# Runs of four matmuls in one chunk, and the sums of two norms one chunk later and one chunk earlier

## The chip, the cores and the metric

One Trainium2 chip, of which the program uses one core. The time is device microseconds for one execution, from start to end, on that core. Shown is the median of three runs; one further execution was profiled.

## The reference

Two transformer blocks after one another, on 256 positions of width 2048, all in float32. Block 1 has a banded attention and a gated linear attention side by side, then a feed-forward of width 5632 with a causal convolution and gelu, then a gate with a side input (`ple`). Block 2 has a sliding-window attention and a stick-breaking attention, two gated branches, and a feed-forward of width 5632 without convolution. Cut to what the change touches:

```python
# block 1
x = x + (gelu(u_gate) * u_val) @ w_ffn_down            # u = conv(rms_norm(x) @ w_ffn_up)
h = rms_norm(x, norm_ple_w)
x = x + sigmoid(h @ w_ple_gate) * (p @ w_ple_proj)
x = rms_norm(x, final_norm_w)
# block 2
h = rmsnorm(x, norm_mix_g);  proj = h @ w_in           # attentions, branches, w_out
x = x + merged @ w_out
x = x + (silu(gate) * up) @ w_ffn_down                 # gate, up = split(rmsnorm(x, norm_ffn_g) @ w_ffn_in)
```

## The kernel before

**Chunks.** Every weight matrix is streamed through as chunks of 128 x 1024 numbers (512 KB), in one list `self.chunks`. A chunk is loaded (`load_ahead`, on SP's queue, up to five ahead) and split in two parts, `hi` (ACT rounds it to float32r, L195) and `lo` (DVE subtracts, L115), up to two chunks ahead of TensorE (three in `ple`), each in one of four buffers (`split`). The activations are split in the same way and stand side by side as 256 columns of hi and 256 of lo.

**Matmuls of a chunk.** A chunk of `job_t` has eight 128 x 128 tiles of weights (two output tiles `m` by four `kk`). Each tile makes two matmuls on L269: its `hi` part against all 512 columns and its `lo` part against the first 256. A hi and a lo result are added when they are evacuated from PSUM (`joined`, L330 on ACT and L115 on DVE). `multiply` sets their order: `runs = (2, 2, 2, 2)` means two tiles with hi, the same two with lo, and so on four times; a run is here one such group, hi and then lo.

**Pairs.** `pair_up(at, alone, odd)` takes a stretch of the list. Its first `alone` chunks stay single, with runs of two tiles. All others are taken two at a time in one run of sixteen tiles: sixteen hi, then sixteen lo; their hi part starts 15 numbers further into its buffer. `odd=True` gives the last single chunk `runs = (4, 2, 2)`, three runs for four. `w_out` of block 1 has two single chunks and `odd=True`. Each feed-forward has 264 chunks (176 of the first matrix and 88 of the second): ten single ones and 127 pairs, both with `odd=False`. The gates and branches of block 2 from the third on (36 pairs) and `w_out_2` (16 pairs) have no single chunk.

**Work between chunks.** After the matmuls of each chunk `step()` goes once through a list of generators (`hot`, the attention chains and others): each issues its instructions up to its next `yield`. `yield AGAIN` means a second go in the same step. What a chunk's `after` appends is first run in the step after the next chunk. Evacuations that need the factor of the norm wait until `self.inv` is set, and two are issued per step (`may_evac`). A chunk that opens a new output tile needs a free PSUM bank out of four; if there is none, `lin_tile` calls `step()` until one is free, with no matmul in between.

**The norms.** The sum over features of a norm is a matmul with ones (`norm_sums`, L394 and L397) of the sums of squares that POOL adds up in `acc` (L359, L361). `norm` yields `wait` times, issues the sum, then in the next step the first half of `rstd` (DVE, ACT with Ln and Exp) and in the step after it the second half (three DVE instructions), with which `inv` is set. `ev_res` starts it for the norm before the feed-forward of either block and for the one before `ple` (`norm_ple_w`). In the first chunks of `ple` the order is: three chunks of the gate's job 0, three of job 1, the fourth of job 0, the projection chunk of job 0, the fourth of job 1.

`norm_between` computes the two norms between the blocks at once: two sums, of `accs[0]` (squares of x before the gain) and `accs[1]` (after it). The first chunks of block 2 are, by `overlap`, `ak` 0 to 2, `av` 0 to 2, `ak` 3, `av` 3, then `aq` 0 and on. `ak` and `av` fill all four PSUM banks.

Of the kernel before, what the change touches and what calls it, by code (L numbers as in the profile page):

```python
# [91 lines left out]
class Builder:  # L92
# [602 lines left out]
    def ev_res(self, k0, src, wname, pool, tag, acc):  # L695

        def ev(m, ps):
            k = k0 + m
            self.add_res(k, ps)
            yield AGAIN  # L700
            x = self.xr[k]
            self.scaled_in(src, k, pool, tag, x, self.vec(wname, k))
            self.sum_squares(acc(), x, k == 0)
            if k == KD - 1:
                self.inv = None
                self.hot.append(self.norm(acc(), wait=2))
            yield
        return ev

# [204 lines left out]
    def ffn(self, wu, wd, conv):  # L914
        nc, a = self.nc, self.a
        h = self.h_ffn
        segs = ((0, 16), (16, 16), (32, 12))
        top = len(self.chunks)
        acc = []
        out = Src(KD)  # L920
        self.h_next = out
        st = {}

        def conv_of(ps, j):
            while not self.may_evac():
                yield
            t = self.joined(ps)
            u = self.ft.tile([P, T], F32, tag="cu", name="cu")
            nc.gpsimd.tensor_tensor(u, t, self.inv[:, :T], ALU.mult)  # L929
            yield  # L930
            if not conv:
                return u
            o = self.ft.tile([P, T], F32, tag="co", name="co", bufs=4)
            self.act(o, u, AF.Identity, scale=self.vec("conv2", j), bias=self.vec("b_ffn_conv", j))
            self.stt(o[:, 1:], u[:, :T - 1], self.vec("conv1", j), o[:, 1:], ALU.mult, ALU.add)
            self.stt(o[:, 2:], u[:, :T - 2], self.vec("conv0", j), o[:, 2:], ALU.mult, ALU.add)
            yield
            return o

        for si, (f0, fn) in enumerate(segs):  # L940
            g = Src(fn)

            def ev_gate(j0):
                def ev(m, ps):
                    o = yield from conv_of(ps, j0 + m)
                    gt = self.ft.tile([P, T], F32, tag="gt", name="gt", bufs=4)
                    self.act(gt, o, AF.Gelu_apprx_tanh if conv else AF.Silu)
                    st[j0 + m] = gt
                return ev

            def ev_val(j0, g=g, f0=f0):
                def ev(m, ps):
                    o = yield from conv_of(ps, KF + j0 + m)
                    j = j0 + m
                    gt = st.pop(j)
                    self.tt(gt, gt, o, ALU.mult, nc.gpsimd if conv else None)
                    self.put_y(g, j - f0, gt)
                return ev

            at = len(self.chunks)  # L960
            for j in range(f0, f0 + fn, 2):
                self.job_t(wu, 0, KD, j // 2, h, ev_gate(j))
                self.job_t(wu, 0, KD, (KF + j) // 2, h, ev_val(j))
            if si == 0:
                self.overlap(at, 4)
            final = si == len(segs) - 1

            def ev_down(k0, final=final):
                def ev(m, ps):
                    self.add_res(k0 + m, ps)  # L970
                    yield
                return ev
            at = len(self.chunks)
            for j in range(KD // 2):
                if not final:
                    ev = ev_down(2 * j)
                elif conv:
                    ev = self.ev_res(2 * j, out, "norm_ple_w", self.xa, "xa", lambda: acc[0])
                else:
                    ev = self.ev_final(2 * j)  # L980
                before = None
                if final and j == 0:
                    def before():
                        acc.append(self.new_acc())
                        self.acc_f = acc[0]
                        if conv:
                            self.open_ple()
                self.job_t(wd, f0, fn, j, g, ev, before=before)
            self.overlap(at, fn // 4)
        self.pair_up(top, 10, odd=False)  # L990


    def open_ple(self):
# [73 lines left out]
    def norm_between(self, accs):  # L1067

        nc = self.nc
        inv = self.const.tile([P, 258], F32, tag="inv", name="inv", bufs=2)
        i1 = self.ft.tile([P, T], F32, tag="inv1", name="inv1", bufs=1)
        m1 = self.ft.tile([P, 258], F32, tag="m1", name="m1", bufs=1)
        yield
        yield
        pb = self.bank2(1)
        p1 = self.norm_sums(accs[0], pb[:, 0], True)  # L1080
        p2 = self.norm_sums(accs[1], pb[:, 1], True)
        yield

        def both(m):
            self.mean_eps(p1, D)(m1)
            nc.vector.tensor_scalar(m, m1, scalar1=EPS, scalar2=None, op0=ALU.mult)
            self.stt(m, p2, 1.0 / D, m, ALU.mult, ALU.add)
        yield from self.rstd(inv, both, 258)
        self.inv = inv
        for _ in range(4):  # L1090
            yield
        yield from self.rstd(i1, lambda m: nc.vector.tensor_copy(m, m1[:, :T]), T)
        for k in range(KD):
            nc.gpsimd.tensor_tensor(self.xr[k], self.xr[k], i1, ALU.mult)
            if k % 2:
                yield
# [368 lines left out]
```

## Time and profile before

| what | value |
|---|---|
| median of 3 runs | 2601.51 us (2599.85 to 2602.99) |
| profiled execution, time | 2602.29 us |
| its span, first to last instruction | 2600.6 us |
| TensorE's matmuls (PE) busy | 2578.5 us, 99% of the span |
| weight loads (PEld) busy | 2239.1 us, 86% |
| DVE, ACT, POOL busy | 65%, 52%, 21% |
| mean granted TensorE clock | 0.998 |

A busy PE is not PE at its peak: matmuls overlap, and the profile models their ends. The pace is read from the distance between the starts of rows. The profiled execution is 0.8 us above the median, and 1.7 us of its time lie outside the span.

### The profile page before, as it was taken

To read this page: it belongs to the slowest core of one execution; us is meant where nothing else is said; L and a number is where in the kernel's file an instruction comes from. 1 tells how busy PE (TensorE), PEld (TensorE's weight loads), DVE (VectorE), ACT (ScalarE), POOL (GpSimd) and SP (SyncE) were. 2 spreads that over 40 slices of the span, in tenths; PEclk is the share of its full clock that TensorE was granted. 3 is DMA by queue.
4 is the path that set the end of the run, shared out by engine and by line. 5 is a ranking of instruction groups with operands and counts; after the bars stand their busy time and mean duration, and the time that the engine had idled before them with its cause. 6 is when DMAs were issued, how large, how long until landed. Compare 5 with 4: busy or idle time off the path is not lost.

```text
span 2600.6 us, 39330 instructions
## 1 busy us (share of the span) xinstructions
PE 2578.5 (99%) x14864; PEld 2239.1 (86%) x14864; DVE 1692.3 (65%) x2241; ACT 1346.4 (52%) x2018; POOL 553.0 (21%) x638
## 2 busy tenths in 40 slices
PE   9999999999999999999999999999999999999997
PEld 7888888888888888888878888888888888888886
DVE  7457677776677667779676665556655555555555
ACT  5545545664466446557555655554554444444443
POOL 4121232220122012346520121112211001100114
PEclk9999999999999999999999999999999999999999
DMA  7556565666566656655545555656555555555553
GB/s 247 155 163 190 168 232 189 194 194 195 190 194 193 195 190 193 224 165 166 167 144 156 154 178 188 194 193 190 185 192 186 188 182 191 192 182 192 185 188 122
DMA packets 133753, 480.38 MB, mean 185 GB/s; under 512 B 15067, under 2 KB 17371, under 8 KB 133436
## 3 DMA queue, kind: packets, MB, share of 16 engines
q1 hardware_dynamic: 132108, 474.45, 57.3%
q8 instruction: 117, 1.92, 0.3%
q0 software_dynamic: 736, 2.36, 0.3%
q10 hardware_dynamic: 720, 1.06, 0.1%
q14 instruction: 72, 0.59, 0.1%
HBM read 475.71 MB, written 2.10 MB: 184 GB/s over the span
## 4 chain that ended last, share of the span: by engine, by line
PE 96%; DVE 1%; POOL 1%; DMA 1%; issue 0%; ACT 0%; DVEq 0%; SPq 0%; ACTq 0%
PE lin L269 87%; PE lin L311 4%; PE lin L309 2%; PE c L269 1%; PE c L792 1%; PE c L742 1%; PE c L779 0%; DMA raw<-in_w_out 0%; DVE lo L115 0%; PE c L1282 0%; DMA raw<-in_w_gk 0%; DVE x L115 0%; POOL x_in L525 0%; PE c L891 0%; PE c L872 0%
## 5 line engine op out<-in xcount | busy, mean ns | idle before, releaser
L115 DVE TENSOR_TENSOR lo<-raw,hi 128x1024 fp32r<-128x1024 f32 (+1 forms) x889 | 1104.0, 1275 | 658.8 <-issue 330.5
L195 ACT CAST hi<-raw 128x1024 fp32r<-128x1024 f32 (+1 forms) x890 | 912.7, 1046 | 480.0 <-PE lin L269 424.7
L269 PE MATMUL lin<-xa,hi 128*128 128x512 f32 x3808 | 985.1, 393 | 0.8 <-DVE xa L118 0.4
L269 PEld LDWEIGHTS lin<-xa,hi 128*128 128x128 f32 x3808 | 668.2, 188 | 107.9 <-issue 2.3
L269 PE MATMUL lin<-g,hi 128*128 128x512 f32 x2592 | 665.0, 394 | 3.4 <-DVE jo L115 3.1
L269 PEld LDWEIGHTS lin<-xa,lo 128*128 128x128 f32 x3808 | 534.5, 188 | 59.9 <-DVE lo L115 5.2
L269 PE MATMUL lin<-xa,lo 128*128 128x256 f32 x3808 | 549.4, 279 | 1.1 <-DVE lo L115 1.1
L269 PEld LDWEIGHTS lin<-g,hi 128*128 128x128 f32 x2592 | 458.3, 188 | 80.8 <-issue 6.1
L269 PEld LDWEIGHTS lin<-g,lo 128*128 128x128 f32 x2592 | 358.8, 188 | 35.0 <-DVE lo L115 0.4
L269 PE MATMUL lin<-g,lo 128*128 128x256 f32 x2592 | 366.8, 279 | 0.0
L929 POOL TENSOR_TENSOR cu<-jo,inv 128x256 f32<-128x256 f32 x176 | 128.2, 749 | 1113.0 <-DVE jo L115 1113.0
L330 ACT COPY jb<-lin 128x256 f32<-128x256 f32 x313 | 113.2, 371 | 70.7 <-PE lin L269 58.4
L118 DVE SCALAR_TENSOR_TENSOR co<-cu,vecs,co 128x255 f32<-128x255 f32 (+1 forms) x176 | 89.7, 531 | 53.1 <-ACT co L112 50.0
L115 DVE TENSOR_TENSOR jo<-lin,jb 128x256 f32<-128x256 f32 x297 | 113.6, 417 | 11.7 <-ACT jb L330 8.9
L112 ACT ACTIVATE co<-cu,vecs 128x256 f32<-128x256 f32 x88 | 52.9, 602 | 103.9 <-POOL cu L929 99.9
L348 ACT CAST g<-gt 128x256 fp32r<-128x256 f32 x88 | 35.6, 404 | 115.1 <-DVE gt L115 89.2
L359 POOL TENSOR_TENSOR sq<-x 128x256 f32<-128x256 f32 x73 | 58.4, 800 | 150.5 <-DVE x L115 150.3
L361 POOL TENSOR_TENSOR acc<-acc,sq 128x256 f32<-128x256 f32 x73 | 89.0, 1219 | 5.7
L115 DVE TENSOR_TENSOR jo<-lin,x 128x256 f32<-128x256 f32 x128 | 53.3, 416 | 29.0 <-PE lin L269 28.8
L112 ACT ACTIVATE xa<-x,vecs 128x256 fp32r<-128x256 f32 x48 | 24.5, 510 | 86.9 <-DVE x L115 86.9
L269 PE MATMUL lin<-m,hi 128*128 128x512 f32 x256 | 62.3, 395 | 0.0
L1180 POOL TENSOR_TENSOR u<-jo,inv 128x256 f32<-128x256 f32 x32 | 24.1, 770 | 175.4 <-DVE jo L115 175.4
(217 smaller groups left out, 1622.9 us busy)
## 6 DMA issues: line engine op xcount, KB each, us to landing
raw<-in_w_ffn_up SPq DMA_DIRECT2D x176, 512.0 KB, 4.3
raw<-in_w_ffn_down SPq DMA_DIRECT2D x176, 512.0 KB, 4.3
raw<-in_w_ffn_in SPq DMA_DIRECT2D x176, 512.0 KB, 4.3
raw<-in_w_out SPq DMA_DIRECT2D x64, 512.0 KB, 4.4
raw<-in_w_aq SPq DMA_DIRECT2D x32, 512.0 KB, 3.7
raw<-in_w_ple_gate SPq DMA_DIRECT2D x32, 512.0 KB, 4.3
raw<-in_w_ga SPq DMA_DIRECT2D x32, 512.0 KB, 3.7
raw<-in_w_gb SPq DMA_DIRECT2D x32, 512.0 KB, 4.1
```

What stands on the lines that cost most here:

```text
L112: self.nc.scalar.activation(out, in_, func, **kw)
L115: (eng or self.nc.vector).tensor_tensor(out, a, b, op)
L118: self.nc.vector.scalar_tensor_tensor(out, in0=in0, scalar=scalar, in1=in1, op0=op0, op1=op1)
L195: self.nc.scalar.copy(hi, r)
L269: self.nc.tensor.matmul(ps[m][:, T:] if lo else ps[m], lhsT=(ch.lo if lo else ch.hi)[:, at:at + P], rhs=src.tile[k][:, :T] if lo else src. ...
L309: self.nc.tensor.matmul(ps[t][:, :wd], lhsT=xl, rhs=wt, start=k == 0, stop=False)
L311: self.nc.tensor.matmul(ps[t][:, :wd], lhsT=xh, rhs=wt, start=False, stop=bool(lo) and k == KD - 1)
L330: self.nc.scalar.copy(b[:n], ps[:n, T:])
L348: self.nc.scalar.copy(t[:, :T], x)
L359: g.tensor_tensor(sq, x, x, ALU.mult)
L361: g.tensor_tensor(acc, acc, sq, ALU.add)
L929: nc.gpsimd.tensor_tensor(u, t, self.inv[:, :T], ALU.mult)
```

## The change

The last of the ten single chunks of block 2's feed-forward gets runs of four, two and two tiles. The sum of the norm before `ple` is issued one step later, and the sums between the blocks one step earlier.

```diff
@@ ev_res
-                self.hot.append(self.norm(acc(), wait=2))
+                self.hot.append(self.norm(acc(), wait=3 if wname == "norm_ple_w" else 2))
@@ ffn
             self.overlap(at, fn // 4)
-        self.pair_up(top, 10, odd=False)
+        self.pair_up(top, 10, odd=not conv)
@@ norm_between
         m1 = self.ft.tile([P, 258], F32, tag="m1", name="m1", bufs=1)
-        yield
         yield
         pb = self.bank2(1)
```

`conv` is true for block 1's feed-forward and false for block 2's.

## Rows read from the trace of the kernel before

**Rows 1.** The page: the chain that ended last by engine; a group of matmuls.

```profile
PE 96%; DVE 1%; POOL 1%; DMA 1%; issue 0%; ACT 0%; DVEq 0%; SPq 0%; ACTq 0%
...
L269 PE MATMUL lin<-xa,lo 128*128 128x256 f32 x3808 | 549.4, 279 | 1.1 <-DVE lo L115 1.1
```

**Rows 2.** Windows of PE: the pairs of either feed-forward; length, busy (matmuls), clock, DMA.

```profile
437.60:1129.40 691.80, 691.80 (x4067) 1.00 0.61 196
...
1871.60:2585.30 713.70, 713.70 (x4066) 1.00 0.56 183
```

**Rows 3.** Timeline of PE, first pair of block 1's feed-forward: start, us.

```profile
437.44 0.39 PE L269 MATMUL lin<-xa,lo 128*128 128x256 f32 x2
437.66 3.80 PE L269 MATMUL lin<-xa,hi 128*128 128x512 f32 x16
...
443.11 3.79 PE L269 MATMUL lin<-xa,hi 128*128 128x512 f32 x16
```

**Rows 4.** The same, last single chunk and first pair of block 2's feed-forward.

```profile
1868.57 0.40 PE L269 MATMUL lin<-xa,lo 128*128 128x256 f32 x2
1868.81 0.62 PE L269 MATMUL lin<-xa,hi 128*128 128x512 f32 x2
...
1871.33 0.40 PE L269 MATMUL lin<-xa,lo 128*128 128x256 f32 x2
1871.57 3.90 PE L269 MATMUL lin<-xa,hi 128*128 128x512 f32 x16
...
1877.19 3.89 PE L269 MATMUL lin<-xa,hi 128*128 128x512 f32 x16
```

**Rows 5.** The same, the chunk with three runs in w_out of block 1.

```profile
322.45 0.40 PE L269 MATMUL lin<-g,lo 128*128 128x256 f32 x2
322.68 1.08 PE L269 MATMUL lin<-g,hi 128*128 128x512 f32 x4
...
325.24 0.39 PE L269 MATMUL lin<-g,lo 128*128 128x256 f32 x2
325.46 3.80 PE L269 MATMUL lin<-g,hi 128*128 128x512 f32 x16
```

**Rows 6.** The same, last attention matmuls of block 2 to its first pair.

```profile
1523.43 0.87 PE L792 MATMUL c<-l,vb 128*64 128x256 f32 x8
...
1525.50 0.39 PE L269 MATMUL lin<-g,lo 128*128 128x256 f32 x2
...
1557.46 3.80 PE L269 MATMUL lin<-g,hi 128*128 128x512 f32 x16
```

**Rows 7.** The same, a wait within the pairs of w_out of block 1.

```profile
342.20 3.87 PE L269 MATMUL lin<-g,hi 128*128 128x512 f32 x16 [0.23 <-DVE x L115]
345.90 2.05 PE L269 MATMUL lin<-g,lo 128*128 128x256 f32 x16
```

**Rows 8.** Timelines of POOL and PE at the norm before ple.

```profile
1140.65 1.59 POOL L361 TENSOR_TENSOR acc<-acc,sq 128x256 f32<-128x256 f32 x1
...
1141.13 0.39 PE L269 MATMUL lin<-xa,lo 128*128 128x256 f32 x2
1142.30 0.70 PE L394 MATMUL c<-acc,ones 128*128 128x256 f32 x2 [0.78 <-POOL acc L361]
```

**Rows 9.** Timelines of POOL, PE and DVE at the norms between the blocks; a window.

```profile
1246.85 1.81 POOL L361 TENSOR_TENSOR accb<-accb,sq 128x256 f32<-128x256 f32 x2
...
1252.57 0.59 PE L394 MATMUL c<-acc,ones 128*128 128x256 f32 x2
...
1254.41 0.43 DVE L404 TENSOR_SCALAR m<-c 128x258 f32<-128x258 f32 x1 [1.26 <-PE c L397]
...
1256.23 1.12 PE L311 MATMUL lin<-lo,g 128*128 128x256 f32 x8
1260.48 0.85 PE L269 MATMUL lin<-g,hi 128*128 128x512 f32 x2 [3.13 <-DVE jo L115]
...
1260.50:1264.10 3.60, 3.60 (x12) 3.07 (x13) 1.39 (x2) 1.36 (x3) 1.35 (x2) 0.55 0.27 108
```

## The prediction

> **What bounds the kernel.** I read the page first. The chain that ended last is 96% PE [rows 1], so time is won only where PE waits or where its matmuls come faster. Waits of PE are few, so the second view is the windows of its busy time, one for the 127 pairs of each feed-forward. Both windows hold the same work (4067 and 4066 matmuls recorded), both at full granted clock, and PE is never idle in them; yet block 1's takes 691.8 us and block 2's 713.7 [rows 2]. Fewer bytes per us move in the slower one, and no engine is waited for. The pairs themselves are slower: by the timeline, from one pair's first row to the next, 443.11 - 437.66 = 5.45 us in block 1 and 1877.19 - 1871.57 = 5.62 us in block 2 [rows 3, 4]. Sixteen hi matmuls last 3.80 us at the first pace and 3.90 at the second.
>
> So TensorE has two paces for the same matmuls. Read along the timeline they are a state that is handed on. A pair passes on the pace it was given. A single chunk alternates: its rows of two lo matmuls last 0.39 us at the fast pace and 0.40 at the slow, in turn, one run fast and one slow, so four runs leave the pace as they found it. What the pairs inherit is the last lo row before them: 0.39 in block 1 and the pairs are fast [rows 3]; 0.40 in block 2 and they are slow [rows 4]. What it is in the hardware the profile doesn't tell; I use it as a state that the rows show.
>
> **The change part by part.** *Three runs in the last single chunk.* No matmul, load or wait is added or removed; 16 matmuls change places. An odd number of runs should hand on the other pace. The trace has one such chunk, in w_out of block 1, and it stands where the new one will: the lo row before it is slow, 0.40 (322.45), as is the one before block 2's last single chunk (1868.57) [rows 4, 5]. It ends with a fast row, 0.39 (325.24), and the pair behind it is fast, 3.80 [rows 5]. The chunk itself takes 325.46 - 322.68 = 2.78 us, against 1871.57 - 1868.81 = 2.76 with four runs [rows 4, 5]: a loss of 0.02. The gain is 127 x (5.62 - 5.45) = 21.6 us by single pairs, 713.7 - 691.8 = 21.9 by windows. I take 21.9. The bounds are 0 (the pace isn't turned) and 21.9. That the faster pace can be fed follows from block 1's feed-forward, which holds it for all 127 pairs with the same loads (DMA share 0.61) and more work on DVE, ACT and POOL [rows 2].
>
> Here a rule speaks against the change. The Trainium skill ("TensorE: Matmul & The Clock Gate", section "Back-to-back issue gap") gives the distance of back-to-back matmuls at the full clock from their columns alone, N/2.4 ns plus about 2.5: 215.8 and 109.2 ns here, 5.20 us for a pair in any order. By it the edit is worth 0 and the sum is 5.0 us. This trace disagrees: the same 32 matmuls take 5.45 and 5.62 us.
>
> Would the norms' edits disturb the entry? They lie before block 2's attention. After its last attention matmuls the second lo row is already fast (0.39), only whole chunks of four runs follow, and the first pair is fast [rows 6]. The edits move whole steps between chunks, so I expect that stretch, and the singles of the feed-forward, to begin as now.
>
> *The norm before ple, one chunk later.* PE comes to the sum behind the chunk whose last lo row starts at 1141.13 and takes 0.22 [rows 3, 8], but POOL ends the last addition at 1140.65 + 1.59 = 1142.24, and the sum starts at 1142.30 [rows 8]. PE loses 1142.30 - 1141.13 - 0.22 = 0.95 us. One chunk later, some 2.76 us, POOL has long ended: 0.9 us won, between 0 (the next lo part is late instead) and 0.95. What is late next is `inv`, by one step: its second half is then issued in the step after the fourth chunk of the gate's job 0. That chunk's evacuations are first tried in the step behind it, when `inv` is set in both versions; so no evacuation is put off and the two jobs' four banks come free as before. Queued behind the delayed DVE and ACT work are the splits of chunks three ahead, which have two chunks of 2.76 us to spare. If that cover were gone, PE would wait for a bank here as it does at the next norm, up to 4.8 us.
>
> *The sums between the blocks, one chunk earlier.* Now PE issues them behind `ak` 3 (1252.57). DVE's first instruction on them starts 1254.41 - 1252.57 = 1.84 us later, and from there to the next matmul it is 1260.48 - 1254.41 = 6.07 us [rows 9]: Ln and Exp, a split, the second half of `rstd`, and the first joined tile, because all four banks are full until `inv` lets `ak` be evacuated. PE's last matmul before it is over at 1256.23 plus 8 x 0.12 (eight in 1.12 us, one lasting 0.28: 0.84/7) = 1257.19 [rows 1, 9]. It waits 3.29 us. Afterwards it has half the clock for a while: the window behind holds 12 matmuls in 3.60 us at 0.55, where six hi and lo at 2.76/8 would take 2.07 [rows 4, 9]: another 1.5 us.
>
> In the new place the sums start behind `av` 2, one chunk earlier, at 1252.57 - 2.76 = 1249.81. POOL's last addition to `accs[1]` ends at 1246.85 + 1.81 = 1248.66 [rows 9], 1.15 us before: a cover that holds if PE comes 0.9 earlier, and more since the second sum comes behind the first. The same chain then ends at 1249.81 + 1.84 + 6.07 = 1257.72; DVE may still be at three splits before it, which I allow 0.4 for. PE, whose work up to there is the same, still needs until 1257.19. A wait of 0.5 to 0.9 is left, I take 0.7: 2.6 us won, and 1.5 for the clock, which I expect not to fall after so short a wait. That is 4.1; bounds 0 (the attention chains give it back) and 4.8. `inv` is set before `aq` 0 in both versions (now by a forced step, then by an ordinary one), so everything behind it keeps its place by chunks, and moves up with PE, whose freed buffers pace the splits.
>
> **Sum.** 21.9 - 0.02 + 0.9 + 4.1 = 26.9 us, so 2602.3 - 26.9 = 2575.4 for the profiled execution. That one was 0.8 above the median, so I forecast 2574.6. Its own range takes the norms at 0 to 5.7, and 1.6 us of spread between runs: 2572 to 2581.
>
> **The rivals.** *The pace isn't turned.* Then only the norms count: 2601.5 - 5.0 = 2596.5. For it: the one chunk that shows the turn is in another stage, with other operands (`g`, not `xa`). The rule of the Trainium skill weighed above would be it, too. Against it: same shapes, same buffers and offsets, the same pace before it, and block 1's feed-forward, whose `xa` pairs are fast behind a fast row [rows 3].
>
> *The pace is turned and lost on the way.* In w_out of block 1 the fast pairs end at a wait of PE: the row at 342.20 has 0.23 us idle, the lo row behind it takes 2.05, and it stays at that [rows 7]. A single wait in the feed-forward, for a late lo part or bank, could do the same. Lost at half way it gives 2574.6 + 11.0 = 2585.6, at the start 2596.5. Against it: neither feed-forward has a wait of PE within its pairs [rows 2].
>
> *A third and slower pace.* In `av` before the norms' wait the lo matmuls come 0.12 us apart, steadily [rows 9], where the slow pairs have (2.05 - 0.28)/15 = 0.118 [rows 1, 7]. If runs of four led into a pace like it, with hi at twice that, a pair would take 16 x 0.36 = 5.76: 127 x 0.14 = 17.8 us lost, 2601.5 + 17.8 - 5.0 = 2614. It decides from (5.2 + 5.0)/127 = 0.08 us per pair on, that is above 5.70. Against it: it is seen only where every matmul has 256 columns.
>
> *The norms' edits turn the entry after all.* Then the 36 pairs of gates and branches turn slow, 36 x 0.17 = 6.1 lost, and the new chunk could turn the feed-forward the wrong way, from fast to slow: 2601.5 + 6.1 - 5.0 = 2602.6.
>
> **Chances.** The forecast has 80%: a state read in four entries (three fast, one slow), with the very chunk shown once. Not turned 10%, lost on the way 5%, entry turned 2%, third pace 3%. From no change a measurement of this kernel tells about 0.2%, 5.2 us. Faster: forecast and lost on the way, 85%. Same: not turned (2596.5 is just within) and entry turned, 12%. Slower: 3%. The range holds the forecast's own and reaches up to where a pace lost half way lies: 2571 to 2586.
>
> **What would show it.** Right: in the last single chunk four hi, four lo, then a last lo row of 0.39; pairs 5.45 us apart from there to the end, 692 us for all; no idle before the sum of the norm before ple; a wait of under 1 us ahead of `aq` 0 and full clock behind it. Wrong: a last lo row of 0.40, or pairs of 5.62; a wait of PE within the pairs with 2.05 behind it; sums that wait for POOL; a forced wait for a bank in ple.

## The result and the profile after

The changed kernel takes 2575.42 us (median of three runs, 2572.91 to 2575.5) against 2601.51 (2599.85 to 2602.99). The ratio is 0.9897, 95% interval 0.9874 to 0.9919: 26.1 us, or 1.0%, faster. The forecast was 2574.6 with a range of 2571 to 2586. The profiled execution took 2575.42, with a span of 2573.7; its counterpart before took 2602.29 with 2600.6. The two spans differ by 26.9 us, and the rest of this section says where they lie.

First the page of the changed kernel: the chain that ended last by engine, and the group that [rows 1] shows of before.

```profile
PE 97%; DVE 1%; POOL 0%; DMA 0%; ACT 0%; issue 0%; SPq 0%; DVEq 0%; ACTq 0%
L269 PE MATMUL lin<-xa,lo 128*128 128x256 f32 x3808 | 542.6, 277 | 2.4 <-DVE lo L115 2.4
```

PE is still what bounds it, and its share has gone up since what stood in the way is shorter. One lo matmul is busy for 277 ns on average where it was 279: small, since the mean is over all stages and over busy times that overlap. The windows of PE over the pairs of either feed-forward say it plainly (length, busy, clock, DMA share, GB/s; compare [rows 2]).

```profile
438.10:1129.90 691.80, 691.80 (x4067) 1.00 0.61 196
1866.70:2558.50 691.80, 691.80 (x4067) 1.00 0.58 189
```

Both feed-forwards now hold their 127 pairs in the same time. By the starts of rows it is 691.73 us in each, and 713.75 in block 2 before: 22.0 us won at the same granted clock. The timeline of PE over the last single chunk and into the pairs answers to [rows 4]:

```profile
1863.70 0.40 PE L269 MATMUL lin<-xa,lo 128*128 128x256 f32 x2
1863.94 1.08 PE L269 MATMUL lin<-xa,hi 128*128 128x512 f32 x4
1864.86 0.63 PE L269 MATMUL lin<-xa,lo 128*128 128x256 f32 x4
1865.33 0.63 PE L269 MATMUL lin<-xa,hi 128*128 128x512 f32 x2
1865.80 0.40 PE L269 MATMUL lin<-xa,lo 128*128 128x256 f32 x2
1866.03 0.62 PE L269 MATMUL lin<-xa,hi 128*128 128x512 f32 x2
1866.49 0.39 PE L269 MATMUL lin<-xa,lo 128*128 128x256 f32 x2
1866.72 3.80 PE L269 MATMUL lin<-xa,hi 128*128 128x512 f32 x16
...
1872.17 3.80 PE L269 MATMUL lin<-xa,hi 128*128 128x512 f32 x16
```

The chunk is entered behind a slow lo row (0.40 at 1863.70), as before, has three runs (the first of four hi), and is left by a fast one (0.39 at 1866.49). The pairs behind it are 1872.17 - 1866.72 = 5.45 us apart instead of 5.62. The chunk itself takes 1866.72 - 1863.94 = 2.78 us, 0.02 more than with four runs. Inside it the runs don't alternate one by one, though. From the first of the four lo matmuls to the next hi it is 1865.33 - 1864.86 = 0.47 us (sixteen take 1.89 at the slow pace and 1.81 at the fast, a quarter of which is 0.47 and 0.45). So this run is slow behind a slow row, the next lo row is slow again (0.40 at 1865.80), and only the last is fast. What the chunk turns, it turns as a whole.

At the norm before `ple` (timelines of PE and POOL, to be set beside [rows 8]):

```profile
1140.79 1.60 POOL L361 TENSOR_TENSOR acc<-acc,sq 128x256 f32<-128x256 f32 x1
...
1144.04 0.41 PE L269 MATMUL lin<-xa,lo 128*128 128x256 f32 x2
1144.29 0.59 PE L394 MATMUL c<-acc,ones 128*128 128x256 f32 x2
```

POOL ends the last addition at 1140.79 + 1.60 = 1142.39, 0.15 later than before; PE comes to the sum 1.90 us after that, and its row has no idle time.

At the norms between the blocks (timelines of POOL, PE and DVE, and a window behind them; [rows 9] are those of before):

```profile
1245.95 1.80 POOL L361 TENSOR_TENSOR accb<-accb,sq 128x256 f32<-128x256 f32 x2
...
1248.86 0.59 PE L394 MATMUL c<-acc,ones 128*128 128x256 f32 x2
...
1254.11 1.23 DVE L115 TENSOR_TENSOR lo<-raw,hi 128x1024 fp32r<-128x1024 f32 x1 [1.88 <-ACT hi L195]
...
1255.30 1.12 PE L311 MATMUL lin<-lo,g 128*128 128x256 f32 x8
1256.99 0.73 PE L269 MATMUL lin<-g,hi 128*128 128x512 f32 x2 [0.57 <-DVE jo L115]
...
1260.00:1264.00 4.00, 4.00 (x25) 3.50 (x24) 2.03 (x3) 1.93 (x2) 0.00 (x0) 1.00 0.77 217
```

The sums start 1.11 us after POOL's last addition (1245.95 + 1.80 = 1247.75). The matmuls ahead of `aq` 0 end at 1255.30 + 8 x 0.12 = 1256.26, and the next starts at 1256.99: a wait of 0.73 where it was 3.29. The clock stays at 1.00 behind it, where before a window of 3.60 us had 0.55.

Laid end to end, by the starts of the first rows of each stage. The cut behind `ple` is at the first `av` matmul, so the three `ak` chunks ahead of it are counted with `ple`:

| stage of the profiled execution | before, us | after, us | difference |
|---|---|---|---|
| up to the end of block 1's pairs | 1129.39 | 1129.88 | +0.49 |
| from there to the first `av` matmul (`ple` and `ak` 0 to 2) | 111.79 | 110.35 | -1.44 |
| first `av` to the first gate pair (norms between, attentions) | 316.29 | 312.36 | -3.93 |
| gate pairs, `w_out_2`, ten single chunks | 314.11 | 314.13 | +0.02 |
| 127 pairs of block 2's feed-forward | 713.75 | 691.73 | -22.02 |
| sum | | | -26.88 |

The first row is code that the change doesn't touch. It comes back in the second: `ple` waits early on for its side input, and the cast of it starts at nearly the same time in both.

```profile
1133.16 0.74 ACT L348 CAST pt<-p_in 128x256 fp32r<-128x256 f32 x2 [6.27 <-DMA p_in<-in_pT]
```

That is before; after, it starts at 1133.30, 0.14 later and not 0.49. So 0.35 of the 1.44 is a wait that merely got shorter because PE came later, and 1.1 is the norm's.

### The profile page after: what moved, and what is told of

It is laid out like the page before. It is cut to its first block, busy times and chain, and to the rows that moved or that the text cites. A ratio compares the mean times of both kernels' runs of the same rounds, so it can differ in the third digit from the quotient of the medians.

```text
span 2573.7 us, 39329 instructions
## 1 busy us (share of the span) xinstructions
PE 2554.6 (99%) x14864; PEld 2227.2 (87%) x14864; DVE 1692.8 (66%) x2241; ACT 1347.3 (52%) x2018; POOL 553.9 (22%) x638
## 4 chain that ended last, share of the span: by engine, by line
PE 97%; DVE 1%; POOL 0%; DMA 0%; ACT 0%; issue 0%; SPq 0%; DVEq 0%; ACTq 0%
PE lin L269 87%; PE lin L311 4%; PE lin L309 2%; PE c L269 1%; PE c L792 1%; PE c L742 1%; PE c L779 0%; DMA x_in<-in_xT 0%; PE c L1281 0%; DVE x L115 0%; DVE lo L115 0%; DMA p_in<-in_pT 0%; PE c L891 0%; PE c L872 0%; PE c L886 0%; PE c L1316 0%
## 5 line engine op out<-in xcount | busy, mean ns | idle before, releaser
L269 PEld LDWEIGHTS lin<-xa,lo 128*128 128x128 f32 x3808 | 528.5, 188 | 60.5 <-DVE lo L115 6.5
L269 PE MATMUL lin<-xa,lo 128*128 128x256 f32 x3808 | 542.6, 277 | 2.4 <-DVE lo L115 2.4
```

The costliest lines, as they stand in the source:

```text
L269: self.nc.tensor.matmul(ps[m][:, T:] if lo else ps[m], lhsT=(ch.lo if lo else ch.hi)[:, at:at + P], rhs=src.tile[k][:, :T] if lo else src. ...
```

## The experiments

**The theory** is the prediction's: the matmuls have two paces; an odd number of runs in a single chunk turns what is handed on; the pairs keep it; the norms' edits win their waits and nothing else. **Its rivals**: the faster pace belongs to the place or the operands (a three-run chunk helps there whatever the pace before it); or the gain came from the norms' edits shifting the entry. A pair is called slow at 5.62 us and fast at 5.45.

### Each part alone

`runs_only` is the kernel before with the three runs:

```diff
-        self.pair_up(top, 10, odd=False)
+        self.pair_up(top, 10, odd=not conv)
```

> Only the three runs of the last single chunk; both norms as before. Handed-on pace: the pairs of block 2's feed-forward come 5.45 us apart, 692 us for all, and the time is 2601.5 - 21.9 = 2579.6. Rival, that the turn needs the shifted norms ahead of it: pairs 5.62 us apart, 2601.

`norms_only` is the changed kernel with that line as it was, so both norms' edits alone:

> Only the two norms; runs of two throughout. Forecast: 0.9 + 4.1 = 5.0 us won, 2596.5, pairs of block 2's feed-forward slow at 5.62 us. Rival, that the attention chains give the norms' part back: 2600 to 2601.

`between_only` and `ple_only` split these two further: the one has only the `yield` in `norm_between` taken out, the other only the later sum before `ple`.

> Only the sums between the blocks one chunk earlier. The wait before aq 0 falls from 3.3 us to 0.5 to 0.9, the clock stays full: 4.1 us won from the end of ple to the first pairs of the gates; PE still waits 0.9 us for POOL ahead of the norm before ple; pairs of the feed-forward slow; 2597.4. Rival, that this part of the gain needs the other norm's shift: under 2 us won.

> Only the sum of the norm before ple one chunk later. PE no longer waits for POOL there: 0.9 us won, 2600.6, and the wait of 3.3 us before aq 0 stays. Rival, that the norm's later factor costs it elsewhere in ple: 2601.5 or more.

| kernel | time, us (before, same chip) | ratio, 95% | `ple`, `ak` 0 to 2 | first `av` to gates | block 2's pairs |
|---|---|---|---|---|---|
| before (its profile) | | | 111.79 | 316.29 | 713.75 |
| runs_only | 2581.29 (2602.29) | 0.9918, 0.9902 to 0.9935 | 111.59 | 317.43 | 691.73 |
| norms_only | 2597.26 (2602.29) | 0.998, 0.9971 to 0.999 | 109.83 | 312.29 | 713.75 |
| between_only | 2598.82 (2602.34), one run | | 111.48 | 312.36 | 713.75 |
| ple_only | 2601.12 (2601.88), one run | | 110.65 | 316.15 | 713.75 |

The parts add up. The runs win 21.0 us by themselves, the norms 5.0, 26.0 together, and both at once won 26.1. In each kernel only the stage moves that its edit belongs to, but for one stage of `runs_only` that is told below: the pairs with the runs, `ple` with the later sum (109.83 and 110.65, against 111.48 to 111.79 with the earlier one), the stage behind the first `av` by 3.9 with the earlier sums. The rival that the norms turn the entry is out: `norms_only` has all 127 pairs slow, `runs_only` all fast. The time of `ple_only` alone wouldn't show its 0.8 us, since the runs of the kernel before reach from 2599.18 to 2604.75 beside it; its stage does.

`runs_only` took 1.7 us more than the 2579.6 expected, and the 21.0 us that it wins are 1.0 short of the 22.0 that its pairs give back. Its stage behind the first `av` is 317.43, 1.1 longer than before's, in code that it doesn't change. The windows behind the wait ahead of `aq` 0 show it, first of `runs_only`:

```profile
1260.00:1264.00 4.00, 3.58 (x11) 0.50 0.36 121
1264.00:1268.00 4.00, 4.00 (x19) 0.72 0.48 131
```

and of the kernel before:

```profile
1260.00:1264.00 4.00, 3.52 (x12) 0.61 0.36 120
1264.00:1268.00 4.00, 4.00 (x24) 0.96 0.45 131
```

After nearly the same wait (3.12 and 3.13 us idle) the clock stays low for longer in one execution than in the other, for 11 + 19 matmuls in 8 us instead of 12 + 24. So the price of that wait isn't fixed: 1.5 us in one profile, some 1.1 more in another. `norms_only` and `between_only`, with the earlier sums, have 1.00 in the same windows, and so has every other profile with the earlier sums just behind this place. So the changed kernel is rid of this loss as well as of the wait. The times fit: ten runs of `norms_only` lie within 1.5 us, thirteen of the kernel before within 5.4; that this wait alone makes the difference is not shown.

### Does it turn, or does it only help?

`two_odd` gives the ninth single chunk three runs as well, on top of the change; `conv_odd` gives block 1's feed-forward three runs, which is entered at the other pace; `first_odd` has the three runs in the second single chunk instead of the last.

```diff
 two_odd    after the line of pair_up, for block 2
+            self.chunks[top + 8].runs = (4, 2, 2)
 conv_odd
+        self.pair_up(top, 10, odd=True)
 first_odd  with odd=False, for block 2
+            self.chunks[top + 1].runs = (4, 2, 2)
```

> As changed, and the ninth single chunk of block 2's feed-forward also has three runs, so that the number of runs is even again (two chunks with a run of four). Handed-on pace, turned by each run: the pairs are slow, 5.62 us, and the time is 2575.4 + 22 = 2597. Rival, that the run of four just ahead of the pairs brings the fast pace by itself: 5.45 us, 2575.

> As changed, and block 1's feed-forward also has three runs in its last single chunk. Handed-on pace: there the entry is fast now, so the same edit turns it slow: block 1's pairs 5.62 us, 714 us for all, time 2575.4 + 22 = 2597. Rival, that a run of four brings the fast pace by itself: block 1's pairs stay at 5.45 us, 2575.

> As changed, but the chunk with three runs is the second of the ten and not the last, ahead of the norm. Handed-on pace: it doesn't matter where the odd chunk stands; the last lo row before the norm is then fast, as in block 1, and the pairs are fast: 692 us, 2575. Rival, that it has to be the chunk next to the pairs: 714 us, 2597.

`two_odd` took 2597.79 us (one run, before 2602.29): all 127 pairs are slow, 713.75. The timeline of PE over its last single chunk:

```profile
1864.07 0.39 PE L269 MATMUL lin<-xa,lo 128*128 128x256 f32 x2
1864.30 1.07 PE L269 MATMUL lin<-xa,hi 128*128 128x512 f32 x4
...
1866.85 0.40 PE L269 MATMUL lin<-xa,lo 128*128 128x256 f32 x2
1867.09 3.90 PE L269 MATMUL lin<-xa,hi 128*128 128x512 f32 x16
```

The very same last chunk, with the same buffers and operands as in the changed kernel, is now entered fast and left slow. `conv_odd` took 2597.36 us (one run): block 1's pairs, fast in every kernel so far, are slow, and block 2's stay fast. Its timeline at the entry of block 1's:

```profile
435.14 0.39 PE L269 MATMUL lin<-xa,lo 128*128 128x256 f32 x2
435.37 1.07 PE L269 MATMUL lin<-xa,hi 128*128 128x512 f32 x4
...
437.22 0.40 PE L269 MATMUL lin<-xa,lo 128*128 128x256 f32 x2
...
437.92 0.40 PE L269 MATMUL lin<-xa,lo 128*128 128x256 f32 x2
438.16 3.90 PE L269 MATMUL lin<-xa,hi 128*128 128x512 f32 x16
```

`first_odd` took 2575.91 us (one run), no different from the change. Behind its three-run chunk come eight chunks of four runs with the sum of a norm among them, and the pace gets through:

```profile
1841.66 0.40 PE L269 MATMUL lin<-xa,lo 128*128 128x256 f32 x2
1841.90 1.08 PE L269 MATMUL lin<-xa,hi 128*128 128x512 f32 x4
...
1866.97 0.39 PE L269 MATMUL lin<-xa,lo 128*128 128x256 f32 x2
1867.19 3.80 PE L269 MATMUL lin<-xa,hi 128*128 128x512 f32 x16
```

Three kernels in which a place-bound effect and a turn give opposite answers, and all three go with the turn. It is not that three runs are good: where the stage is entered fast they cost the same 22 us that they win here.

That the chunk turns the pace is shown; that it does so because three is odd is not. Runs that alternate one by one would be slow, fast and slow in `conv_odd`, but its second lo row is slow too (0.40 at 437.22). Every chunk of three runs here is also one with a run of four, and no kernel tried has the one without the other (a chunk in one run of eight, say, or in two of four). So it may as well be the run of four that turns the pace.

### Where else the pace comes from

`no_shift` is the changed kernel without the 15 numbers by which a pair's hi part starts further into its buffer:

```diff
-FURTHER = (15, 0)
+FURTHER = (0, 0)
```

> As changed, but the hi parts of paired chunks start at the same place in their buffers as those of single ones (shift of 0 for 15). If the shift is what lets a pair keep its pace, pairs turn it as single runs do, and come 5.45 and 5.62 us apart in turn: 11 us lost in each feed-forward, 3 in the gates, about 2598. Rival, that the length of the run keeps the pace: 2575.

It took 2593.13 us (one run), which is neither of the two numbers expected. The pairs are neither fast nor slow but change from one to the next; PE's timeline in the gate pairs:

```profile
1703.95 3.82 PE L269 MATMUL lin<-xa,hi 128*128 128x512 f32 x16
1707.61 2.05 PE L269 MATMUL lin<-xa,lo 128*128 128x256 f32 x16
1709.50 3.84 PE L269 MATMUL lin<-g,hi 128*128 128x512 f32 x16
1713.17 1.98 PE L269 MATMUL lin<-g,lo 128*128 128x256 f32 x16
1714.99 3.82 PE L269 MATMUL lin<-g,hi 128*128 128x512 f32 x16
```

Sixteen lo take 1.89 us (1709.50 - 1707.61) and then 1.82 (1714.99 - 1713.17), and the hi parts 3.66 and 3.67, between the fast 3.63 and the slow 3.73. The pairs of a feed-forward take 700.7 us in either block, 8.9 more than at the fast pace. Twice that, 17.9, is nearly the 17.7 us between this kernel and the changed one; the pairs elsewhere change it little in sum (1.35 us less up to block 1's pairs, 0.85 more from the first gate pair to block 2's). So without the 15 numbers the lo parts of the pairs are slow and fast in turn, and with them they aren't. That the pairs pass a pace on depends on how their buffers are laid out, which the prediction had taken as given.

`w2_even` puts two single chunks of four runs in front of the pairs of `w_out_2`. Those pairs were slow in every kernel so far but `no_shift`, though the gate pairs ahead of them are fast. The trace of the kernel before has it already: its last gate pair starts with 3.80 at 1748.10, the first pair of `w_out_2` with 3.90 at 1753.54. The edit is:

```diff
-        self.pair_up(at, 0)
+        self.pair_up(at, 2)
```

> As changed, and w_out_2, whose 16 pairs are slow, gets two single chunks of four runs each ahead of 15 pairs. Handed-on pace: it is entered fast, eight runs leave it fast, and 15 pairs win 0.17 us each, 2.6 us less 0.2 for the singles. Then the feed-forward behind it is entered fast as block 1's ple is, and three runs there turn its pairs slow: 714 us, 2595. Rival, that these pairs are slow by themselves, since their parts start 32 numbers further: nothing changes in either, 2575.

2575.98 us (one run). Its first two lo rows show where the pace goes:

```profile
1747.48 1.98 PE L269 MATMUL lin<-xa,lo 128*128 128x256 f32 x16
...
1749.77 0.40 PE L269 MATMUL lin<-m,lo 128*128 128x256 f32 x2
...
1750.47 0.40 PE L269 MATMUL lin<-m,lo 128*128 128x256 f32 x2
...
1754.85 3.90 PE L269 MATMUL lin<-m,hi 128*128 128x512 f32 x16
```

The gates end fast (1.98), the first `m` lo row is slow and the second is slow again, where runs of two tiles otherwise alternate, as they do from there on. The pace is turned where the moving operand changes from `xa` to `m`. Block 2's feed-forward is entered slow after it all the same, and stays fast behind its three runs.

The weights of `w_out_2` are also the only ones whose split parts lie 32 numbers further into their buffers than those of the other streamed matrices (the 24 is for the resident projection of `ple` alone). `m_same` takes these 32 away, with both norms' edits and four runs in the feed-forward:

```diff
-MORE_OFF = {"w_out_2": 32, None: 24}
+MORE_OFF = {None: 24}
```

> The norms as changed; the parts of w_out_2's chunks start at the same place in their buffers as those of the pairs before (no further 32 numbers); no run of four in block 2's feed-forward. If the jump of the place turns the pace, w_out_2's 16 pairs are now fast, 16 x 0.17 = 2.8 us won against the changed kernel; the feed-forward is then entered from fast pairs, as ple is, and four runs in each of ten chunks leave it fast: 2575.4 - 2.8 = 2572.6. Rival, that the change of operands (xa to m) turns it: w_out_2 slow, feed-forward slow, 2597.

2597.13 us, ratio 0.9982 (0.9973 to 0.9992): the pairs of `w_out_2` are slow from the first on, as with the 32, and so are those of the feed-forward. The offset isn't what turns it; that expectation failed and its rival held. Whether it is the operand itself or something else that changes with it (the weights' matrix, the results' use) no run separates.

`wout12` keeps all that and gives `w_out` of block 1 twelve single chunks for two, `pair_up(at, 12, odd=True)`, so that a wait of PE falls among single chunks and not among pairs [rows 7].

> As the run without the further 32 numbers, and w_out of block 1 has twelve single chunks for two, the last with three runs, so that its wait of PE falls among single chunks and ten pairs come behind it. After a wait among single chunks two runs are slow and then they alternate (ple shows it), so the three runs end fast: ten pairs at 5.45 us for 5.62, less 0.1 us: 1.6 us more won, 2571.0. Rival, that the wait leaves the other pace: ten slow pairs, 2572.7.

2597.33 us, ratio 0.9984 (0.9975 to 0.9993), no gain over `m_same`. With the pairs gone from there the wait is another and earlier one (0.43 us idle at 326.61, for a lo part), and the rows behind it go on alternating. The last single chunk was entered fast and so left slow:

```profile
350.88 0.39 PE L269 MATMUL lin<-g,lo 128*128 128x256 f32 x2
351.10 1.07 PE L269 MATMUL lin<-g,hi 128*128 128x512 f32 x4
...
353.66 0.40 PE L269 MATMUL lin<-g,lo 128*128 128x256 f32 x2
353.90 3.90 PE L269 MATMUL lin<-g,hi 128*128 128x512 f32 x16
```

Its expectation of fast pairs failed, but it is one more entry that the three runs turn from fast to slow, in a third stage.

`w2_odd_ff_even` asks whether a three-run chunk turns a stage's pace where the change has none: three runs in the second single chunk of `w_out_2`, four in the feed-forward, and both norms' edits.

```diff
-        self.pair_up(at, 0)
+        self.pair_up(at, 2, odd=True)
```

> The norms as changed; w_out_2 keeps its further 32 numbers and gets two single chunks, the second with three runs; no run of four in block 2's feed-forward. By the run with two singles of four runs each, which ended slow, seven runs end fast: 15 pairs at 5.45 us, 2.6 us won. The feed-forward is then entered from fast pairs: as ple, and fast, 2573; or as it was entered before, and slow, 2595.

2594.79 us (one run), 2.5 us under `norms_only`; from the first gate pair to the feed-forward's pairs it takes 311.45 us, `norms_only` 314.11. The timeline of PE, at the entry of `w_out_2` and of the feed-forward:

```profile
1751.24 0.40 PE L269 MATMUL lin<-m,lo 128*128 128x256 f32 x2
...
1753.34 0.40 PE L269 MATMUL lin<-m,lo 128*128 128x256 f32 x2
...
1754.04 0.39 PE L269 MATMUL lin<-m,lo 128*128 128x256 f32 x2
1754.26 3.80 PE L269 MATMUL lin<-m,hi 128*128 128x512 f32 x16
...
1836.43 0.40 PE L269 MATMUL lin<-xa,lo 128*128 128x256 f32 x2
...
1837.13 0.40 PE L269 MATMUL lin<-xa,lo 128*128 128x256 f32 x2
...
1864.06 3.90 PE L269 MATMUL lin<-xa,hi 128*128 128x512 f32 x16
```

All 15 pairs of `w_out_2` are fast, 15 x 0.17 = 2.6 us by the pairs. The feed-forward behind them starts with two slow lo rows, though the last `m` pair was fast, and ends in slow pairs. Where `m` gives way to `xa` the pace is set to slow, behind fast pairs here as behind slow ones in the kernel before. That is why the feed-forward needs its own three runs. The changed kernel with the same two single chunks in `w_out_2` should then take about 2575.4 - 2.6 = 2572.8 us; that is an estimate, as this version was not run.

## Why the prediction was right

- **The three runs turn the pace** (21.9 by windows, 0.02 lost in the chunk). Measured: 22.02 in the pairs, 2.78 us for the chunk, last lo row 0.39, pairs 5.45 apart up to the end. Shown for the chunk as a whole, by five more chunks of three runs in the experiments: slow to fast in `first_odd` and `w2_odd_ff_even`, fast to slow in `two_odd`, `conv_odd` and `wout12`. Not shown is the reason that the prediction gives, that runs alternate and three is odd: within the chunk they don't alternate. The number held because the forecast rested on a chunk that had been seen to turn [rows 5]. Nor do 16 matmuls change places in it, as the prediction has it, but four of its 16: two lo and two hi.
- **The norm before ple** (0.9). Measured: no idle ahead of the sum, the stage 1.44 shorter, of which 0.35 is the side input's wait, so 1.1 won. Nothing was late in its place: no row of PE from the sum to the projection chunk has idle time before it.
- **The sums between the blocks** (2.6 for the wait, 1.5 for the clock, 4.1). Measured: 3.93. The chain from the sums to `aq` 0 took 1256.99 - 1248.86 = 8.13 us, forecast 1.84 + 6.07 + 0.4 = 8.31. A split does stand in it, as allowed for: a lo part at 1254.11 of 1.23 us, ahead of the second half of `rstd`. The wait left is 0.73, forecast 0.7. The 1.5 us for the clock is the term that holds least: with the sums in the old place it was 1.1 us more in `runs_only` than in the profile it was read from.
- **The entry is not touched by the norms.** 314.11 and 314.13 us from the first gate pair to the feed-forward's pairs, and two slow lo rows at the start of the feed-forward in both (from 1843.94 before, from 1839.07 after).
- **Against the rule weighed there.** The prediction took from the Trainium skill ("TensorE: Matmul & The Clock Gate", section "Back-to-back issue gap") a formula by which the order of runs couldn't matter. That section calls it the gap of an isolated matmul and says that in a stream of weight loads and matmuls both set the distance, so the rule was weaker than the prediction made it. The runs here don't follow the formula's 5.20 us: 32 matmuls of the same columns at the same granted clock take 5.45, 5.62 or, in `no_shift`, alternately 5.55 and 5.49 us (from 1703.95, 1709.50 and 1714.99).

One more sentence of the prediction was too wide: that a pair passes on the pace it was given. `no_shift` shows that without the hi part's 15 numbers it doesn't, and `w2_even` and `w2_odd_ff_even` that the chain breaks where the moving operand changes to or from `m`. The slow pairs of `w_out_2` behind fast gate pairs, in the trace of the kernel before, spoke against it, and the prediction's four entries leave them out. Neither touches the stretch from the three-run chunk to the end of its pairs, which is why the number held.

What stays open is what the two paces are. The rows show that they depend on the order of runs and on where a part starts in its buffer, and that they can change where another tensor begins to move; no run here says by what mechanism.

## What to carry to other kernels

Where a bound engine is never idle, compare the pace of the same instructions in two stages by the starts of their rows; 3% over 700 us hid in a page that says 99% busy. If the pace alternates, find what hands it on and set it at a cheap place before a long uniform stretch, by what the pace is there, since the same edit at the other pace loses as much. And an instruction that ends a wait chain is worth issuing as soon as its inputs are sure to be there: one chunk earlier (2.76 us) took away 2.6 us of wait, and with it a stretch in which the granted clock was 0.55.

## What the runs showed that was not expected

- Where `m` begins or ends as the moving operand the pace is slow (`xa` to `m` at 1748.68 in the changed kernel, where the fast gate pairs end; `m` to `xa` behind fast pairs in `w2_odd_ff_even`, behind slow pairs in the changed kernel), while from `g` to `xa` in the gate pairs the fast pace goes through.
- A chunk of three runs turns the pace, but its own lo rows go slow, slow, fast when it is entered slow and slow, slow, slow when it is entered fast.
- Without the 15 numbers the pairs change pace in turn, 700.66 us for the 127 pairs of block 1: 8.9 more than all at 5.45, 13.1 less than all at 5.62.
- After about the same idle time, 3.12 and 3.13 us, the clock in the next 4 us was 0.50 in one execution and 0.61 in the other, and 0.72 and 0.96 in the 4 us after that; after 0.57 us idle it stayed at 1.00.
